# A recurrence's output projection and weight splits become steps of its own list; four products move to GpSimd

## The chip, the cores and the metric

One Trainium2 chip, one core of it. The metric is the device time of one execution of the whole program in microseconds (us). TensorE is called PE below, its weight loads PEld, VectorE DVE, ScalarE ACT, GpSimd POOL and the engine that issues most transfers SP.

## What is computed

The program is one inference step of a four-layer decoder trunk on 320 tokens (256 of a prompt, 64 of 8 samples), width 1024. Each layer is a token mixer (RG-LRU, Mamba-2, RWKV-7, RG-LRU) and then an MLP with squared ReLU. The change lies wholly in the third layer's mixer:

```python
def step(S, inp):                               # WKV recurrence, 16 heads of 64
    r_t, k_t, v_t, kk_t, a_t, w_t = inp
    sa = jnp.einsum("bhvk,bhk->bhv", S, kk_t)
    S = (S * w_t[:, :, None, :] - sa[..., None] * (kk_t * a_t)[:, :, None, :]
         + v_t[..., None] * k_t[:, :, None, :])
    return S, jnp.einsum("bhvk,bhk->bhv", S, r_t)
...
bonus = (jnp.sum(r_h * k_h * r_k, axis=-1, keepdims=True) * v_h).reshape(bsz, L, D_MODEL)
out = ((o + bonus) * g).astype(u.dtype)         # o: the steps' outputs, normed per head
return out @ w_out, u[:, -1], S_fin.astype(wkv0.dtype)
...
x = x + out.astype(x.dtype)
x = x + sqrelu_mlp(rmsnorm(x, p["norm_ffn"][layer]), ...)
```

## The kernel before

Everything is held feature-major, [128 partitions, 8 tiles, 320 tokens]. Weights come from HBM in chunks of 128x1024 f32 (512 KB) through three `wraw` buffers. Each chunk is split in two fp32r parts: ACT writes `whi` (a rounded copy), DVE writes `wlo` (the rest). There are three buffers of each, so a chunk's parts may be written when the matmuls of the third chunk before it have read theirs. A product with such a weight is three matmuls of 320 columns (whi with the high part of the activation, whi with the low part, wlo with the high part).

The recurrence (`wkv`, L1345) works on eight pairs of heads. For each pair there are chunks of 64 tokens: four of the prompt and one of the samples. Generators make its steps: `scores` and `operands` (products of the pair's tensors), `inverse` (a triangular inverse by doubling, blocks 1, 2, 4 ... 32; it needs `t`, a masked copy of `ar`, from block 2 on), `chain` (the four prompt chunks one after another), `chain_sample` (the samples' states: `spread` of vt and of sa, a product with the decay `dend`, then a transfer out), `output` and `finish` (norm, bonus `bs * vf`, gate, split into y's high part `ylw` and low part `yav`). The last two pairs are also prepared here.

What sets the order of all this is a planner, `Weave` (L326). Each step says which engine it wants, for how many ns by a table in the code, and which PSUM banks (six called `b`, one double bank `iu`). The planner keeps a clock for each engine, takes the step that could start first, and by a rank (`RANK`) among equals. What it takes is written out in that order and pinned: the engines run these instructions in program order. Instructions that aren't pinned are placed among them by the framework's scheduler, with a priority where the code gives one.

The output projection stands behind the planner's run. Its eight chunks (`OUT_CHUNKS`: four that hold pairs 0 to 3 of 256 output columns each, two that hold pairs 4 and 5 of 512, two that hold pairs 6 and 7 of 512) make 24 sums of [128, 320] in three PSUM banks, 192 matmuls in all, and each sum is added to the residual `x`. Three of the eight chunks are split as planned steps late in the recurrence (`weights`), the other five beside the projection, by `fill`:

```python
po = bank("b", m % 3)
for k in range(k0, k1):
    mm3(po[:, :N], w[0][:, k - k0, c], ...)
with tc.high_priority(60):
    V.tensor_tensor(x[:, m], x[:, m], po[:, :N], op=ALU.add)
if k1 == NT:
    nxt.tile(m)
```

`nxt.tile(m)` prepares the MLP's input from the finished tile m: ACT writes a square `nsq` (the first goes to `nacc` itself) and the scaled high part `xh`, DVE adds the square to `nacc` and writes the low part `xl`. The MLP's first product (`main_ps`) uses PSUM that the recurrence's banks held, so its first matmul waits for the last add to `x`.

## Time and profile before

| what | value |
|---|---|
| three runs | 1758.85, 1759.35, 1761.85 us, median 1759.35 |
| the profiled execution | 1755.34 us, of which the span 1753.3 |
| busy over the span | PE 97%, DVE 66%, ACT 56%, POOL 1% |
| recurrence, first matmul to the projection's first | 1024.41 to 1154.86 us |
| projection, first to last matmul | 1154.86 to 1185.03 us |
| MLP's first matmul | 1186.39 us |

All stretches below are us from the span's start. A row of the views by stretch gives each engine's busy time with the number of its instructions, then the granted share of TensorE's clock (1.00 is 2.4 GHz, 0.50 is 1.2 GHz). In the chain of waits the time is followed back from the last instruction, each piece under the line and engine that held it; "issue" is time in which the engine waited for nothing that the profile shows.

### The profile page before, as it was taken

The page shows a single profiled execution, that of the slowest core. Times are in us where ns is not written, and L with a number is a line of the kernel's source. Part 1 is how long each engine was busy: PE and PEld are TensorE (multiplying, and loading weights), DVE is VectorE, ACT ScalarE, POOL GpSimd, SP SyncE. Part 2 cuts the span into 40 slices and gives each one's busy share as a digit, 9 for nine tenths or more (in the row PEclk, how much of TensorE's full clock was granted, in tenths as well). Part 3 has the DMA queues.
Part 4 walks back from the last instruction along what each step waited for, and adds up shares of the span by engine and source line. Part 5 has one row for each costly group of instructions (what it writes and reads, how often), then busy time and mean ns, then how long its engine had stood idle before and what let it go on. Part 6 is the DMA issues. An engine that isn't in the chain of part 4 may idle for free.

```text
span 1753.3 us, 35969 instructions
## 1 busy us (share of the span) xinstructions
PE 1693.4 (97%) x15018; PEld 1635.1 (93%) x15018; DVE 1150.3 (66%) x1964; ACT 978.0 (56%) x1608; POOL 17.7 (1%) x36
## 2 busy tenths in 40 slices
PE   8999999989999999999999989899999999999997
PEld 7999999979999989999998977789999999999997
DVE  7975544499978976565467577786554469755444
ACT  7854443378857855553338566655543368554432
POOL 0000000000000000000000000000000000000000
PEclk9999999999999989999999999999999999999999
DMA  5444454545665534545434302134444444454452
GB/s 185 144 137 156 146 154 146 201 134 171 216 200 168 195 125 142 152 136 181 146 116 129 113 21 73 46 120 134 154 146 153 148 134 147 136 153 147 150 151 90
DMA packets 69746, 249.77 MB, mean 142 GB/s; under 512 B 9072, under 2 KB 11536, under 8 KB 67536
## 3 DMA queue, kind: packets, MB, share of 16 engines
q1 hardware_dynamic: 65040, 225.29, 41.5%
q0 software_dynamic: 2960, 18.89, 2.7%
q10 hardware_dynamic: 1584, 3.29, 0.5%
q8 instruction: 118, 1.93, 0.4%
q14 instruction: 44, 0.36, 0.1%
HBM read 233.52 MB, written 13.92 MB: 141 GB/s over the span
## 4 chain that ended last, share of the span: by engine, by line
PE 88%; DVE 7%; ACT 2%; issue 2%; DMA 1%; DVEq 0%; ACTq 0%
PE main_ps L498 22%; PE main_ps L500 22%; PE main_ps L499 22%; PE ps_b L1377 6%; PE aux_ps L499 2%; PE aux_ps L498 2%; PE aux_ps L500 2%; DVE wlo L495 1%; PE aux_ps L768 1%; DVE xc L792 1%; ACT whi L494 1%; PE ps_b L498 1%; PE ps_b L499 1%; PE ps_b L500 1%; PE ps_iu L1377 1%
## 5 line engine op out<-in xcount | busy, mean ns | idle before, releaser
L494 ACT ACTIVATE whi<-wraw 128x1024 fp32r<-128x1024 f32 x398 | 420.9, 1059 | 608.3 <-PE main_ps L499 512.4
L495 DVE TENSOR_TENSOR wlo<-wraw,whi 128x1024 fp32r<-128x1024 f32 x398 | 486.2, 1223 | 368.9 <-ACT whi L494 359.9
L498 PE MATMUL main_ps<-xh,whi 128*128 128x320 f32 x1664 | 521.4, 313 | 16.1 <-ACT whi L494 7.8
L499 PE MATMUL main_ps<-xl,whi 128*128 128x320 f32 x1664 | 518.8, 312 | 0.0
L500 PE MATMUL main_ps<-xh,wlo 128*128 128x320 f32 x1664 | 516.4, 310 | 0.9 <-DVE wlo L495 0.9
L498 PEld LDWEIGHTS main_ps<-xh,whi 128*128 128x128 f32 x1664 | 314.4, 189 | 18.4 <-ACT whi L494 8.0
L499 PEld LDWEIGHTS main_ps<-xl,whi 128*128 128x128 f32 x1664 | 314.3, 189 | 2.1 <-issue 0.4
L500 PEld LDWEIGHTS main_ps<-xh,wlo 128*128 128x128 f32 x1664 | 314.3, 189 | 2.0 <-DVE wlo L495 1.4
L500 PE MATMUL main_ps<-hh,wlo 128*128 128x320 f32 x768 | 237.2, 309 | 0.9 <-DVE wlo L495 0.9
L498 PE MATMUL main_ps<-hh,whi 128*128 128x320 f32 x768 | 237.0, 309 | 0.5 <-ACT whi L494 0.5
L499 PE MATMUL main_ps<-hl,whi 128*128 128x320 f32 x768 | 236.9, 309 | 0.0
L500 PEld LDWEIGHTS main_ps<-hh,wlo 128*128 128x128 f32 x768 | 144.0, 187 | 1.4 <-DVE wlo L495 1.4
L498 PEld LDWEIGHTS main_ps<-hh,whi 128*128 128x128 f32 x768 | 144.0, 187 | 0.8 <-ACT whi L494 0.8
L499 PEld LDWEIGHTS main_ps<-hl,whi 128*128 128x128 f32 x768 | 144.0, 187 | 0.0
L678 DVE SCALAR_TENSOR_TENSOR fr<-main_ps,nrs 128x640 f32<-128x640 f32 x64 | 52.7, 824 | 78.5 <-PE main_ps L500 78.5
L498 PE MATMUL aux_ps<-hh,whi 128*128 128x320 f32 x256 | 79.0, 309 | 0.0
L500 PE MATMUL aux_ps<-hh,wlo 128*128 128x320 f32 x256 | 79.0, 309 | 0.0
L499 PE MATMUL aux_ps<-hl,whi 128*128 128x320 f32 x256 | 79.0, 309 | 0.0
L495 DVE TENSOR_TENSOR hl<-fh,hh 128x640 fp32r<-128x640 f32 x64 | 52.8, 825 | 13.1 <-ACT hh L494 13.1
L851 DVE SCALAR_TENSOR_TENSOR cv<-sxb,k_b,cv 128x344 f32<-128x344 f32 x96 | 51.6, 569 | 0.8 <-ACT cv L849 0.8
L680 ACT ACTIVATE fh<-fr 128x640 f32<-128x640 f32 x64 | 47.3, 739 | 7.3 <-DVE fr L678 7.3
L662 DVE TENSOR_TENSOR x<-x,main_ps 128x320 f32<-128x320 f32 x56 | 24.8, 483 | 36.9 <-PE main_ps L500 36.9
(446 smaller groups left out, 2828.2 us busy)
## 6 DMA issues: line engine op xcount, KB each, us to landing
wraw<-in_wall SPq DMA_DIRECT2D x405, 512.0 KB, 3.7
ss<-in_s POOLq DMA_DIRECT2D x8, 1024.0 KB, 6.8
o_ssm_s<-ss POOLq DMA_DIRECT2D x8, 1024.0 KB, 4.3
acb<-acs_d SPq DMA_DIRECT2D x8, 640.0 KB, 3.9
wx<-in_k SPq DMA_DIRECT2D x8, 256.0 KB, 3.7
o_wkv_s<-wx SPq DMA_DIRECT2D x8, 256.0 KB, 2.7
o_ssm_p<-sp_o POOLq DMA_DIRECT2D x8, 128.0 KB, 4.3
wraw<-in_wlora SPq DMA_DIRECT2D x2, 512.0 KB, 3.7
```

What stands on the lines that cost most here:

```text
L494: S.activation(hi, src, AF.Copy)
L495: V.tensor_tensor(lo, src, hi.bitcast(F32), op=ALU.subtract)
L498: T.matmul(out, wh, ah, start=start, stop=False)
L499: T.matmul(out, wh, al, start=False, stop=False)
L500: T.matmul(out, wl, ah, start=False, stop=stop)
L662: ins = V.tensor_tensor(x[:, i], x[:, i], half(pt, m)[:, :N], op=ALU.add)
L678: V.scalar_tensor_tensor(r, pt[:, :, :N], 0.0, b2(prep.rs), op0=ALU.max, op1=ALU.mult)
L680: S.activation(h, r, AF.Square)
L768: T.matmul(pt[:, :NCV], w4[:, h % 4, s], xc[:, h, :NCV], start=True, stop=True)
L792: V.tensor_tensor_scan(xc[:, h, :NCV], ra[:, h], ix[:, h], 0.0, op0=ALU.mult, op1=ALU.add)
L851: V.scalar_tensor_tensor(out, src[:, k:k + NCV], w[k], out, op0=ALU.mult, op1=ALU.add)
L1377: return lambda *a, **k: tc.keep_in_program_order(fn(*a, **k))
```

## The change

The planner learns of a fourth engine, POOL, and of two kinds of step: `PM` (a PE step that changes between the recurrence's 64x64 matmuls and full ones, at 130 ns more) and `DV2` (a DVE step that reads two operands from SBUF), which it keeps from overlapping with POOL steps on its own clocks.

Four products a pair, 32 in all, go from DVE to POOL: the masked copy `t` (now a step `first` of its own, with a mark `m_t1` that the inverse waits for at block 2), the spread of vt, the samples' states times `dend`, and `bs * vf`. All eight chunks' loads and splits are planned steps (from the third pair's inverse on, at the earliest). The projection is eight planned generators, `project_out`; its adds to `x` lose their priority, are pinned, and any of the six banks may hold a sum. The `nxt.tile(m)` calls stand in a step `next_operand` but are not pinned. Several `RANK` values differ.

```diff
-    LAG = {"PE": 225, "ACT": 53, "DVE": 53, "SP": 0}
+    LAG = {"PE": 225, "ACT": 53, "DVE": 53, "POOL": 95, "SP": 0}
+    KIND = {"PM": "PE", "DV2": "DVE"}
+    SWITCH = 130
...
+                if ns and eng == "PE" and kind != self.mode:
+                    at += self.SWITCH
+                if kind in ("DV2", "POOL"):
+                    at = max(at, self.port)
...
-            RANK = (-27, -31, 0, -2, 21, 13, 36, -41, 30)
+            RANK = (-27, -31, -1, -9, 21, 20, 36, -55, 30, 30)
...
+            def first(g, ar, t):
+                yield "POOL", 680, ()
+                PG.tensor_tensor(t, ar, bc(vk("woff1t"), ND), op=ALU.mult)
+                wv.reach(g.m_t1)
...
-                yield "DVE", 420, ()
-                exv = spread(f"wexv{p % 2}", g.vt[:, j])
+                yield "POOL", 560, ()
+                exv = spread(PG, f"wexv{p % 2}", g.vt[:, j])
...
-                yield "DVE", 690, ()
-                PV.tensor_tensor(k0, k0, dend[:, p, 4:12].unsqueeze(2).to_broadcast([P, NB, 64]), op=ALU.mult)
+                yield "POOL", 1080, ()
+                PG.tensor_tensor(k0, k0, dend[:, p, 4:12].unsqueeze(2).to_broadcast([P, NB, 64]), op=ALU.mult)
...
+                yield g.m_ak
+                yield "POOL", 700, ()
+                PG.tensor_tensor(bs[:, p], bs[:, p], vf[:, p], op=ALU.mult)
...
-                for _ in range(3):
-                    yield gs[6].m_inv
+                yield prepared[7]
+                yield gs[2].m_inv
+                for j in range(len(jobs)):
+                    if j >= 3:
+                        yield w_out[j - 3]
                     raw = raw_chunk()
+                    yield "SP", 2500, ()
...
+            def project_out(j):
+                k0, k1, n, m0 = jobs[j]
+                for k in range(k0, k1):
+                    yield gs[k].m_fin
+                yield w_in[j]
...
+                    i, = yield "PM", 0, ("b",)
+                    po = bank("b", i)
+                    for k in range(k0, k1):
+                        if (k - k0) % 2 == 0:
+                            yield "PM", 882, ()
...
+                    yield "DVE", 490, ()
+                    PV.tensor_tensor(x[:, m], x[:, m], po[:, :N], op=ALU.add)
+                    wv.give("b", i)
+                    if k1 == NT:
+                        wv.add(200, next_operand(m))
...
-            for k0, k1, n in OUT_CHUNKS:
...
-                        with tc.high_priority(60):
-                            V.tensor_tensor(x[:, m], x[:, m], po[:, :N], op=ALU.add)
```

What this does to the order, at three places. **Where the projection begins, on PE.** `ylw`, `yav` are y's parts; rows of 64x64 are the recurrence's. Before, the projection's first matmuls stand behind all but two rows of the recurrence:

```order
L1377 MATMUL ps_b3_10627<-kr_9282,wsn12_11686 64x64 x2
L1377 MATMUL ps_b3_10627<-gbt1_10699,wsa13_11776 64x64 x2
L498 MATMUL ps_b1_10604<-ylw_11656,whi_13464 128x320
L499 MATMUL ps_b1_10604<-yav_11657,whi_13464 128x320
L500 MATMUL ps_b1_10604<-ylw_11656,wlo_13465 128x320
L1377 MATMUL ps_b5_10650<-kr_9282,k_c_9272 64x320 x2
```

Now they begin right behind the last pair's first prompt chunk:

```order
L1393 MATMUL ps_b0_10603<-kr_9282,wx_10597 64x2x8 x12
L1393 MATMUL ps_b5_10650<-vt1_10766,ht1_10938 64x64 x2
L1393 MATMUL ps_b5_10650<-wsa10_11408,bt1_11100 64x64 x2
L1393 MATMUL ps_b3_10627<-ylw_11675,whi_12073 128x320
L1393 MATMUL ps_b3_10627<-yav_11676,whi_12073 128x320
L1393 MATMUL ps_b3_10627<-ylw_11675,wlo_12074 128x320
```

Of the recurrence's 2792 matmuls 2788 stood ahead of the projection's first, now 2706; of the projection's 192, 7 stood ahead of the recurrence's last, now 120 (the first 60 in one piece), and 72 stand behind it.

**Where the projection ends, on DVE.** `x` are the adds to the residual, `nacc` and `xl` belong to `nxt.tile`, the `wlo` rows of L495 and L510 split the MLP's first chunks. Before, the last four adds and what follows:

```order
L1785 TENSOR_TENSOR x_72<-x_72,ps_b1_10604 128x320
L640 SCALAR_TENSOR_TENSOR xl_9268<-x_72,k_cm_73,xh_9267 128x320
L1785 TENSOR_TENSOR x_72<-x_72,ps_b2_10626 128x320
L1785 TENSOR_TENSOR x_72<-x_72,ps_b0_10603 128x320
L572 TENSOR_TENSOR nacc_9266<-nacc_9266,nsq_14259 128x320
L640 SCALAR_TENSOR_TENSOR xl_9268<-x_72,k_cm_73,xh_9267 128x320
L1785 TENSOR_TENSOR x_72<-x_72,ps_b1_10604 128x320
```

Now, up to the last add:

```order
L510 TENSOR_TENSOR wlo_14382<-wraw_14379,whi_14381 128x1024
L587 TENSOR_TENSOR nacc_9266<-nacc_9266,nsq_14284 128x320
L655 SCALAR_TENSOR_TENSOR xl_9268<-x_72,k_cm_73,xh_9267 128x320
L587 TENSOR_TENSOR nacc_9266<-nacc_9266,nsq_14295 128x320
L655 SCALAR_TENSOR_TENSOR xl_9268<-x_72,k_cm_73,xh_9267 128x320
L1393 TENSOR_TENSOR x_72<-x_72,ps_b0_10603 128x320
L587 TENSOR_TENSOR nacc_9266<-nacc_9266,nsq_14301 128x320
L655 SCALAR_TENSOR_TENSOR xl_9268<-x_72,k_cm_73,xh_9267 128x320
L1393 TENSOR_TENSOR x_72<-x_72,ps_b5_10650 128x320
L587 TENSOR_TENSOR nacc_9266<-nacc_9266,nsq_14313 128x320
L655 SCALAR_TENSOR_TENSOR xl_9268<-x_72,k_cm_73,xh_9267 128x320
L1393 TENSOR_TENSOR x_72<-x_72,ps_b4_10649 128x320
```

The split of the MLP's third chunk, `wlo_14382`, and what belongs to two finished tiles have moved ahead of the last three adds. On PE the projection's end and the MLP's beginning now read:

```order
L1393 MATMUL ps_b4_10649<-ylw_13906,whi_14215 128x320
L1393 MATMUL ps_b4_10649<-yav_13907,whi_14215 128x320
L1393 MATMUL ps_b4_10649<-ylw_13906,wlo_14216 128x320
L513 MATMUL main_ps_14342<-xh_9267,whi_14345 128x320
L514 MATMUL main_ps_14342<-xl_9268,whi_14345 128x320
```

`wlo_14216` is the projection's eighth chunk, and `wlo_14382`, three chunks later, is written into its buffer: it waits for the last matmul of the projection.

**Where the recurrence begins, on POOL.** Before, three copies are all that POOL does here:

```order
L1363 COPY ali0_10589<-k_c_9272 128x320
L1363 COPY ali1_10590<-k_c_9272 128x320
L1363 COPY ali2_10591<-k_c_9272 128x320
L443 DMA k_a1_16473<-in_k_a1 128x320
L826 DMA o_lru<-ob_16471 128x288
```

Now an instruction named ISA, which the build adds, and the products stand behind them:

```order
L1378 COPY ali2_10591<-k_c_9272 128x320
L1393 ISA
L1393 TENSOR_TENSOR wt10_10663<-war0_10661,k_c_9272 128x320
L1393 TENSOR_TENSOR wt11_10700<-war1_10698,k_c_9272 128x320
L1393 TENSOR_TENSOR bs_9284<-bs_9284,vf_9283 128x320 x2
L1393 TENSOR_TENSOR wx_10597<-vt0_10703,k_c_9272 128x256
```

The 32 products follow each other in one fixed order on POOL from there.

## Rows read from the trace of the kernel before

**Rows 1.** The page, busy time: engine, us (share of the span), instructions.
```profile
PE 1693.4 (97%) x15018; PEld 1635.1 (93%) x15018; DVE 1150.3 (66%) x1964; ACT 978.0 (56%) x1608; POOL 17.7 (1%) x36
```
**Rows 2.** Busy by stretch: stretch, length, PE, PEld, DVE, ACT, POOL, clock, DMA, GB/s.
```profile
1024.00:1145.00 121.00, 107.57 (x4022) 92.43 (x4023) 89.48 (x225) 80.40 (x241) 0.00 (x0) 0.99 0.17 54
1145.00:1155.00 10.00, 9.47 (x201) 6.85 (x200) 9.20 (x23) 7.58 (x27) 0.00 (x0) 1.00 0.28 86
```
**Rows 3.** Chain of waits, 1024 to 1145 us, shares by engine and line.
```profile
by line: PE ps_b L1377 72.6%; issue 11.0%; PE ps_iu L1377 7.5%; DVE whh L1377 2.0%; ACT wut L1377 1.6%; DVE wu L1377 0.8%; ACT gsq L1377 0.8%; ACT wxs L1377 0.7%; DVE wt L1377 0.4%; DVE gkt L1377 0.4%; DVE wsn L1377 0.4%; ACT wsa L1377 0.4%
```
**Rows 4.** Chain of waits, 1145 to 1185 us, shares by engine and line.
```profile
by line: PE ps_b L1377 27.0%; PE ps_b L498 24.4%; PE ps_b L499 23.2%; PE ps_b L500 22.8%; issue 1.4%; DVE nacc L572 1.2%; ACT wxs L1377 0.6%; ACT wsa L1377 0.6%; DVE x L1785 0.1%
```
**Rows 5.** DVE groups, 1024 to 1166 us: busy us, mean ns | idle before.
```profile
L1377 DVE TENSOR_TENSOR wx<-wx,dend 128x512 f32<-128x512 f32 x8 | 5.5, 690 | 0.2
L1377 DVE TENSOR_TENSOR wt<-war,k_c 128x320 f16<-128x320 f16 x8 | 3.9, 485 | 0.9 <-ACT war L1377 0.9
L1377 DVE TENSOR_TENSOR bs<-bs,vf 128x320 f32<-128x320 f32 x8 | 3.8, 480 | 0.0
L1377 DVE TENSOR_TENSOR wx<-vt,k_c 128x256 f32<-128x256 f32 x8 | 3.3, 415 | 0.0
```
**Rows 6.** Timeline of POOL: start, us, what.
```profile
1021.15 1.76 POOL L1363 COPY ali<-k_c 128x320 f32<-128x320 f32 x3 [375.59 <-DVE kk L1303]
```
**Rows 7.** Chain of waits in order of time, first doubling product.
```profile
1030.19 0.16 PE ps_iu L1377 x14
```
**Rows 8.** Timeline of PE around the projection's end.
```profile
1184.89 0.31 PE L499 MATMUL ps_b<-yav,whi 128*128 128x320 f32 x1
1185.03 0.30 PE L500 MATMUL ps_b<-ylw,wlo 128*128 128x320 f32 x1
1186.39 0.38 PE L498 MATMUL main_ps<-xh,whi 128*128 128x320 f32 x1 [1.05 <-DVE x L1785]
...
1191.01 0.39 PE L499 MATMUL main_ps<-xl,whi 128*128 128x320 f32 x1
1191.76 0.42 PE L500 MATMUL main_ps<-xh,wlo 128*128 128x320 f32 x1 [0.36 <-DVE wlo L495]
```
**Rows 9.** Timeline of DVE at the same place.
```profile
1179.00 1.23 DVE L495 TENSOR_TENSOR wlo<-wraw,whi 128x1024 fp32r<-128x1024 f32 x1 [0.46 <-ACT whi L494]
1180.14 1.28 DVE L1785 TENSOR_TENSOR x<-x,ps_b 128x320 f32<-128x320 f32 x3
...
1184.90 0.48 DVE L572 TENSOR_TENSOR nacc<-nacc,nsq 128x320 f32<-128x320 f32 x1
1185.31 0.55 DVE L640 SCALAR_TENSOR_TENSOR xl<-x,k_cm,xh 128x320 fp32r<-128x320 f32 x1
1185.77 0.48 DVE L1785 TENSOR_TENSOR x<-x,ps_b 128x320 f32<-128x320 f32 x1
```
**Rows 10.** Timeline of ACT at the same place.
```profile
1185.49 0.45 ACT L570 ACTIVATE nsq<-x 128x320 f32<-128x320 f32 x1
1185.85 1.04 ACT L494 ACTIVATE whi<-wraw 128x1024 fp32r<-128x1024 f32 x1
...
1187.16 0.55 ACT L639 ACTIVATE xh<-x,k_cm 128x320 fp32r<-128x320 f32 x1
```
**Rows 11.** Busy by stretch, as in rows 2, around two falls of the clock.
```profile
367.00:374.00 7.00, 2.91 (x20) 2.65 (x19) 6.74 (x16) 4.20 (x11) 0.00 (x0) 1.00 0.13 29
374.00:381.00 7.00, 5.47 (x21) 5.50 (x21) 6.66 (x12) 6.97 (x14) 0.00 (x0) 0.51 0.61 171
1080.00:1084.00 4.00, 2.99 (x137) 2.68 (x132) 3.21 (x9) 2.83 (x10) 0.00 (x0) 1.00 0.01 4
1084.00:1088.00 4.00, 4.00 (x80) 2.22 (x75) 2.10 (x7) 1.43 (x5) 0.00 (x0) 0.57 0.00 0
```
**Rows 12.** Timeline: a pair's variance product on PE, and its `ylw` on ACT.
```profile
1150.26 0.71 PE L1377 MATMUL ps_b<-gsq,k_c 64*64 64x320 f32 x4
...
1156.97 0.47 ACT L1377 ACTIVATE ylw<-cen 128x320 fp32r<-128x320 f32 x1 [0.22 <-DVE cen L1377]
```

More of the change, by code (lines that the diff above doesn't have):

```diff
@@ L404, in run @@
             at, _, task, took = best
-            eng, ns, _ = task.ask
+            kind, ns, _ = task.ask
+            eng = self.KIND.get(kind, kind)
+            if ns and eng == "PE":
+                self.mode = kind
+            if kind in ("DV2", "POOL"):
+                self.port = at + ns
             for tag, i in took:
@@ L1317, in prepare_steps @@
             wv.give("b", i)
-        yield "DVE", 820, ()
+        yield "DV2", 820, ()
         V.tensor_tensor_scan(L, vk("wkvreset"), lwp, 0.0, op0=ALU.mult, op1=ALU.add)
@@ L1422, in __init__ @@
                                             kr[:, 0, i], kr[:, 1, i]))
-                    for nm in ("ready", "a", "gbt", "vt", "ak", "ht", "gkt", "bt", "inv", "used", "o", "os", "out", "fin", "k0"):
+                    for nm in ("ready", "a", "gbt", "vt", "ak", "ht", "gkt", "bt", "inv", "used", "o", "os", "out", "fin", "k0", "t1"):
                         setattr(self, "m_" + nm, Mark())
@@ L1487, in inverse @@
                 PS.activation(ar, g.ali, AF.Copy)
-                yield "DVE", 490, ()
                 t = buf(f"wt1{j}", [P, ND, 64], F16)
-                PV.tensor_tensor(t, ar, bc(vk("woff1t"), ND), op=ALU.mult)
+                wv.add(g.i * 10 + RANK[1], first(g, ar, t))
                 u = None
@@ L1601, in chain_sample @@
                 both(pO, sa, g.gbt[:, j], False, True)
-                yield "DVE", 420, ()
-                exs = spread(f"wexs{p % 2}", sa)
+                yield "DV2", 420, ()
+                exs = spread(PV, f"wexs{p % 2}", sa)
                 yield "DVE", 220, ()
@@ L1763, in wkv, with next_operand @@
+            def next_operand(m):
+                yield "ACT", 930, ()
+                nxt.tile(m)
+                yield "DV2", 1040, ()
             prepared = {p: Mark() for p in (6, 7)}
@@ L1773, in wkv @@
             wv.add(75 + RANK[8], weights())
+            for j in range(len(jobs)):
+                wv.add(75 + RANK[9] + j, project_out(j))
             wv.run()
[L1775 to L1787 removed]
     prep = Prep("norm_mix0")
```

65 lines of the change are left out of this document (36 added, 29 removed).

## The prediction

> **What bounds the kernel now.** I read the page first [rows 1]: PE is busy in 97% of the span, and DVE in two thirds of it. That average says little of this change, which touches one stage, so the stretches of that stage come next [rows 2]. In the recurrence proper, 1024 to 1145 us, PE is busy for 107.57 of 121 us, DVE for 89.48, ACT for 80.40, POOL for nothing. From 1145 us on PE is full (9.47 of 10). The chain of waits tells what PE's idle time hangs on. In the body 72.6 + 7.5 = 80.1% of it is PE itself, 11.0% is "issue", and the remaining 8.9%, or .089 x 121 = 10.8 us, is DVE and ACT together [rows 3]. From 1145 to 1185 us the PE lines alone make 97.4%, and 2.6% of 40 us, about 1 us, is anything else [rows 4]. So the body has 10.8 us that faster DVE work could touch at most, the projection about 1 us, and the hand-over to the MLP a gap that can be read instruction by instruction [rows 8 to 10].
>
> **The change part by part.** *Four products a pair leave DVE.* They measured .485, .415, .690 and .480 us, eight each: 8 x 2.07 = 16.6 us [rows 5], 18.5% of DVE's 89.48. What this frees is DVE's queue. Of the products themselves the chain's listed lines hold only `wt`, .4% of 121, or .5 us [rows 3]; the rest of the gain must come from chain steps (`whh`, `wu`, `gkt`, `wsn`) that no longer stand behind a product. In exchange `t` and the spread of vt become two hand-overs to another engine, on an engine whose only rows here are three copies in 1.76 us, .59 each, with one input [rows 6]. Five more weight chunks' `wlo` come into the list, at a pitch of 1.14 us (1179.00 to 1180.14 [rows 9]), and so give 5.7 of the 16.6 us back. DVE would then have about 79 of 121 us, ACT with five more `whi` of 1.04 [rows 10] about 86, and PE still is the busiest. The gain can't exceed the 10.8 us; a loss is possible, since each of eight inverses waits for a POOL product that may be longer than .485: eight times, say, .6 us gives +5. I take -2.5, nearest to the listed `wt` row and about a fifth of the whole share, because the products' own rows are so little of the chain. Kept for the range: -10.8 to +5.
>
> *POOL's first product* has cover. POOL is free at 1021.15 + 1.76 = 1022.91 [rows 6], and the first doubling product, which needs `t`, runs at 1030.19 [rows 7]: 7.3 us for the added ISA instruction and one product. Cost nothing; if the two take longer, the excess is paid once.
>
> *Projection matmuls move forward.* 120 instead of 7 of the 192 stand ahead of the recurrence's last matmul. They could fill PE's idle time, but they move into a stretch where PE hardly has any [rows 2, 4]: of the 2.6% I expect half a microsecond, -.5 (0 to -1). The 130 ns changes of matmul kind exist on the planner's clock; no row shows such a cost, and the mixed stretch from 1145 us holds PE at 97.4% all the same.
>
> *The last pair's y.* Its parts are needed 24 matmuls behind its variance product in the new order, 24 x .14 = 3.4 us by the pitch of [rows 8]. Before, the way from such a product to `ylw` took 1156.97 - 1150.26 = 6.7 us with DVE as loaded as it was [rows 12]. So PE waits between 0 and 3.3 us there, and for the eighth chunk's `wlo`, which stands behind adds on the same queue. I take a third, +1.1, because fewer operations stand between now.
>
> *The hand-over to the MLP* is the main term. Before, the last projection matmul starts at 1185.03, the last add at 1185.77, and the MLP's first matmul at 1186.39: 1.36 us [rows 8, 9]. The adds came early, since their priority put them ahead of the tiles' preparation. Now they are pinned, and the split of the MLP's third chunk and two tiles' `nacc` and `xl` stand ahead of the last three adds on DVE. `wlo_14382` is written over the chunk that the projection's last matmul reads, and its `whi` over one that the last but one reads, so this piece of DVE's queue can't move until the projection has ended. From the start of that last matmul: its `whi` ends at about +1.25 (the matmul before it ends, then 1.04 [rows 10]); `wlo` 1.14 more, to +2.39; then `nacc` .41 (1184.90 to 1185.31), `xl` .46 (to 1185.77) [rows 9], both twice, 1.74 in all, so the add to the first of the three tiles starts at +4.13. Then each add sends its tile through ACT and back before the next add may go: add .48 [rows 9], a hand-over of about .1, `nsq` at a pitch of .36 (1185.49 to 1185.85), `xh` .55 [rows 10], and `xl` .46: 1.95 a round. Two rounds bring the last add to +8.05. From an add's start to the MLP's first matmul it is .62 (1185.77 to 1186.39): +8.7 where it was 1.36, so 7.3 us more, and 8.1 if DVE comes to this place .8 late with the splits of the two chunks before. One thing is given back: before, PE waited at 1191.76 for the second chunk's `wlo` (.75 us from start to start instead of .14 [rows 8]), and that chunk is split by then now: -.6. Net +6.7 to +7.5, and I take +7.1. Nothing hides this: PE has no other work ahead of the MLP.
>
> *The clock behind it.* Where PE was busy for 2.91 of 7 us at clock 1.00, the following stretch shows .51 with 5.47 us busy; where it was busy for 2.99 of 4 us, the next four show .57 [rows 11]. These are TensorE's two levels, 2.4 and 1.2 GHz, mixed in the slice. The second cost 4.00 x .43 = 1.7 us of PE time, the first 5.47 x .49 = 2.7. An idle hole of 8.7 us is likely to bring such a fall to the MLP's first matmuls. I take +1.7, range 0 to +2.7.
>
> **The sum**: -2.5 - .5 + 1.1 + 7.1 + 1.7 = +6.9 us. The profiled execution took 1755.34, so this one would take 1762.2; it lay 4.0 below the median of the runs, 1759.35, which gives 1766.2. I forecast 1766.
>
> **The rivals.** *The relief is larger than the hole.* If the chain's DVE and ACT steps are late mainly by queueing, taking a fifth of DVE's load away could clear most of the 10.8 us. For it: the many short DVE steps between PE's (`whh` alone 2.0% [rows 3]) and DVE's 74% load in the body [rows 2]. Against it: DVE idles for 31 of the 121 us, and of 16.6 us moved 5.7 come back. It decides from a relief of 5.9 us on: the time is then under 1762.9. With the full 10.8 it is 1766.2 - 8.3 = 1757.9, no change; if in addition the clock doesn't fall behind the hole (-1.7), y is never late (-1.1), the hole is at its lower end (-.4) and the projection gains its whole microsecond (-.5), it is 1754.2, faster.
>
> *POOL and DVE block each other.* The change itself keeps these products apart from DVE's steps with two operands in SBUF, by its planner's clocks; but the engines run by semaphores, and nothing in the program enforces that distance. If one in four of the 32 products holds a DVE step, or is held by one, for as long as a product took on DVE (mean 2.07 / 4 = .52 [rows 5]), and each such hold reaches PE, it is 32 x .25 x .52 = +4.2, so 1770.4. For it: DVE's 74% load leaves few gaps. Against it: no row of before has both engines at work, so this one is open; POOL's work is in one fixed order, and its products read tensors that are ready long before.
>
> The Trainium skill (SBUF — State Buffer, section Who interferes with whom) has a rule for this: a DVE instruction with two SBUF inputs contends with a GpSimd instruction that reads SBUF, and whichever issues first keeps the shared ports for its whole length while the other fully blocks. By that rule this rival is the rule's own price wherever the planner's clocks miss; if they always hit, it costs nothing. No run here shows it yet.
>
> *The change doesn't do what it says*, in that the adds and `nxt.tile` don't run in the written order: the order of instructions on DVE is fixed in the built program, so I give this nothing.
>
> **How the numbers follow.** A chance of .50 for the forecast, .32 for the relief, .18 for the ports. The forecast and the ports are slower by over 0.2% (3.5 us, about what a measurement of this kernel can tell from no change), above 1762.9: .68. Of the relief's .32 I give .22 to a time within 0.2%, 1755.8 to 1762.9, and .10 to faster. For the range, all terms at their favourable ends give 1759.35 + (-10.8 - 1.0 + 0 + 6.7 + 0) = 1754.3, and at their other ends 1759.35 + (5 + 0 + 3.3 + 7.5 + 2.7) = 1777.9. Neither is likely as a whole. 1757 leaves a tenth out below, 1773 a tenth above.
>
> **What would show it.** The start-to-start gap between the projection's last matmul and the MLP's first: 8.7 to 9.5 us instead of 1.36, with DVE's three last adds each about 2 us behind the other and idle time ended by ACT between them; it is wrong if the gap is under 4. A stretch of clock near .5 right behind. DVE's busy time from the recurrence's first matmul to 1145 us down by some 10 us or more, while the chain's share on DVE and ACT falls only from 8.9 to about 7%; below 4% the relief has won. The "issue" share should stay near 11%. Products on POOL that start as soon as their inputs are there, and DVE rows with two SBUF operands no longer than before; such rows growing to more than a microsecond would mean the ports. The first `t` should end before the matmuls that stood at 1030.19 want it. The largest error would be in the relief, which is the only term that rests on a share and not on single instructions.

## The result, and the profile after

The changed kernel takes 1768.99 us (median of five runs, 1768.14 to 1771.52), the kernel before 1758.85 in the same comparison: a ratio of 1.0057, with a 95% interval from 1.0043 to 1.0071. It is slower by 10 us. 1766 was forecast, within 1757 to 1773.

The profiled execution has a span of 1766.4 us where that of before had 1753.3, 13.1 us more. Read from stage to stage, the difference comes to: .9 us ahead of the recurrence (its first matmul starts at 1025.30 instead of 1024.41, in code that the change doesn't touch), 2.2 us from there to the projection's last matmul (162.8 instead of 160.6), 8.45 us in the gap behind it, and 1.6 us from the MLP's first matmul on. The page's busy times, as in [rows 1]:

```profile
PE 1696.3 (96%) x15018; PEld 1639.0 (93%) x15018; DVE 1138.3 (64%) x1932; ACT 978.6 (55%) x1608; POOL 46.1 (3%) x68
```

The products have moved: POOL is busy for 28 us more and DVE for 12 us less. The gap is on PE's timeline, which answers to [rows 8]:

```profile
1187.96 0.31 PE L1393 MATMUL ps_b<-yav,whi 128*128 128x320 f32 x1
1188.11 0.30 PE L1393 MATMUL ps_b<-ylw,wlo 128*128 128x320 f32 x1
1197.92 0.61 PE L513 MATMUL main_ps<-xh,whi 128*128 128x320 f32 x1 [9.51 <-DVE x L1393]
1198.33 0.47 PE L514 MATMUL main_ps<-xl,whi 128*128 128x320 f32 x1
1198.60 0.47 PE L515 MATMUL main_ps<-xh,wlo 128*128 128x320 f32 x1
...
1203.04 0.31 PE L514 MATMUL main_ps<-xl,whi 128*128 128x320 f32 x1
1203.19 0.31 PE L515 MATMUL main_ps<-xh,wlo 128*128 128x320 f32 x1
```

From the projection's last matmul to the MLP's first PE waits 9.81 us from start to start (1.36 before), and what ended the wait is an add to `x` on DVE. Then the matmuls follow each other every .27 us (1198.33 to 1198.60), and from 1203 on every .15. The stretches around the gap, columns as in [rows 2], show why:

```profile
1188.00:1198.00 10.00, 0.49 (x4) 0.26 (x3) 8.59 (x17) 5.12 (x11) 0.00 (x0) 0.73 0.42 122
1198.00:1203.00 5.00, 5.00 (x19) 5.00 (x20) 1.01 (x2) 0.80 (x2) 0.00 (x0) 0.51 0.02 3
1203.00:1208.00 5.00, 5.00 (x38) 5.00 (x37) 1.23 (x1) 1.71 (x2) 0.00 (x0) 1.00 0.18 32
```

PE was busy for .49 of 10 us, and in the 5 us behind it the granted clock was .51: TensorE's lower level, 19 matmuls where the next 5 us hold 38. What DVE did in those 10 us, to be held against [rows 9]:

```profile
1189.64 0.88 DVE L1393 TENSOR_TENSOR x<-x,ps_b 128x320 f32<-128x320 f32 x2
1190.44 1.22 DVE L510 TENSOR_TENSOR wlo<-wraw,whi 128x1024 fp32r<-128x1024 f32 x1
1191.58 0.48 DVE L587 TENSOR_TENSOR nacc<-nacc,nsq 128x320 f32<-128x320 f32 x1
...
1193.30 0.48 DVE L1393 TENSOR_TENSOR x<-x,ps_b 128x320 f32<-128x320 f32 x1
1194.38 0.49 DVE L587 TENSOR_TENSOR nacc<-nacc,nsq 128x320 f32<-128x320 f32 x1 [0.59 <-ACT nsq L585]
1194.83 0.55 DVE L655 SCALAR_TENSOR_TENSOR xl<-x,k_cm,xh 128x320 fp32r<-128x320 f32 x1
1195.30 0.48 DVE L1393 TENSOR_TENSOR x<-x,ps_b 128x320 f32<-128x320 f32 x1
...
1197.30 0.48 DVE L1393 TENSOR_TENSOR x<-x,ps_b 128x320 f32<-128x320 f32 x1
```

This is the piece of the written order that the section on the change showed: the split of the MLP's third chunk at 1190.44, then `nacc` and `xl` of two tiles, and three adds that stand 2.00 us apart (1193.30, 1195.30, 1197.30), each round with a wait for ACT.

### The profile page after: what moved, and what is told of

Read it like the earlier page. It is cut to its first block, busy times and chain, and to the rows that moved or that the text cites. A ratio compares the mean times of both kernels' runs of the same rounds, so it can differ in the third digit from the quotient of the medians.

```text
span 1766.4 us, 35983 instructions
## 1 busy us (share of the span) xinstructions
PE 1696.3 (96%) x15018; PEld 1639.0 (93%) x15018; DVE 1138.3 (64%) x1932; ACT 978.6 (55%) x1608; POOL 46.1 (3%) x68
## 4 chain that ended last, share of the span: by engine, by line
PE 87%; DVE 7%; issue 2%; ACT 2%; DMA 1%; DVEq 0%; ACTq 0%; POOLq 0%
PE main_ps L513 22%; PE main_ps L515 22%; PE main_ps L514 22%; PE ps_b L1393 7%; PE aux_ps L514 2%; PE aux_ps L513 2%; PE aux_ps L515 2%; DVE wlo L510 1%; PE aux_ps L783 1%; DVE xc L807 1%; DMA k_b<-in_k_b 1%; PE ps_iu L1393 1%; PE st_ps L1116 0%; PE nrm_ps L610 0%; ACT whi L509 0%
## 5 line engine op out<-in xcount | busy, mean ns | idle before, releaser
L509 ACT ACTIVATE whi<-wraw 128x1024 fp32r<-128x1024 f32 x393 | 415.4, 1058 | 599.0 <-PE main_ps L514 519.7
L510 DVE TENSOR_TENSOR wlo<-wraw,whi 128x1024 fp32r<-128x1024 f32 x393 | 480.3, 1223 | 373.0 <-ACT whi L509 364.1
L510 DVE TENSOR_TENSOR hl<-fh,hh 128x640 fp32r<-128x640 f32 x64 | 52.8, 825 | 12.7 <-ACT hh L509 12.7
L509 ACT ACTIVATE hh<-fh 128x640 fp32r<-128x640 f32 x64 | 47.4, 741 | 2.0
```

The lines of the kernel that those rows point to most:

```text
L509: S.activation(hi, src, AF.Copy)
L510: V.tensor_tensor(lo, src, hi.bitcast(F32), op=ALU.subtract)
```

## Experiments on the gap

**The adds first.** In the kernel `tailfix` the list, the early splits and the POOL products stay, and only the end is changed:

```diff
-                    PV.tensor_tensor(x[:, m], x[:, m], po[:, :N], op=ALU.add)
+                    if k1 == NT:
+                        with tc.high_priority(60):
+                            V.tensor_tensor(x[:, m], x[:, m], po[:, :N], op=ALU.add)
+                    else:
+                        PV.tensor_tensor(x[:, m], x[:, m], po[:, :N], op=ALU.add)
...
                 for m in range(m0, m0 + n // P):
+                    if j == 7 and m - m0 in (1, 3):
+                        fill(1 + (m - m0) // 2)
```

> The changed kernel with the last eight adds to x given back their priority and unpinned, and the split of the MLP's first two chunks asked for beside the last projection chunk; the list, the early splits and the POOL products stay. In the changed kernel's trace PE stands still for 9.81 us from start to start between the projection's last matmul and the MLP's first (1.36 before), and the MLP's first 18 matmuls then run at a pitch of .267 instead of .147 us, 2.2 us more. Theory (the hole by the order of DVE's last adds): the gap falls to about 1.4 us, the clock stays at 1.00, a wait of up to 1 us for the second chunk's wlo comes back, and the time falls by 9 to 10 us to 1759 or 1760. Rival (the MLP can't use an earlier start, since its weights' splits or the tiles' low parts come late anyway): the gap only moves to the MLP's third and following matmuls, time 1765 or more. Either way the body (first recurrence matmul to last projection matmul, 162.8 us against 160.6 before) stays as it is in the changed kernel.

Measured: 1760.55 us, the kernel before 1760.68 in the same comparison, ratio 1.0002 (.9990 to 1.0014). PE's timeline of this kernel:

```profile
1191.19 0.30 PE L1393 MATMUL ps_b<-ylw,wlo 128*128 128x320 f32 x1
1192.16 0.38 PE L513 MATMUL main_ps<-xh,whi 128*128 128x320 f32 x1 [0.67 <-DVE x L1820]
1192.39 0.31 PE L514 MATMUL main_ps<-xl,whi 128*128 128x320 f32 x1
1192.53 0.31 PE L515 MATMUL main_ps<-xh,wlo 128*128 128x320 f32 x1
```

The gap is .97 us, and the matmuls behind it run at .15 us. By the ratios, 1.0057 against 1.0002, the end of the projection cost 9.7 us. The expected 9 to 10 came, so the loss of the change lies there, and all the rest of it, the list, the early splits and POOL, adds up to nothing measurable (by this ratio's interval between 1.8 us less and 2.5 more). Two things of the expectation didn't come: PE has no wait for the second chunk's `wlo`, and the stretch from the recurrence's first matmul to the projection's last is 165.5 us in this profile, not the 162.8 of the changed kernel (the section on the products takes this up).

**Only the priority.** `addsfirst` has the first half of that diff without the two calls of `fill`.

> The changed kernel with only the priority of the last eight adds given back; the split of the MLP's first chunk isn't asked for early. On DVE wlo of that chunk now stands behind all tiles' nacc and xl. Theory (the start of the MLP is the sum of DVE's order, whatever it is): the first MLP matmul follows at 1.4 us or less, but the third, which reads that wlo, waits for about an xl, four times nacc and xl (.46 + 4 x .87 = 3.9 us) and the split (1.2 us), so it comes some 5 us late, at 6 to 7 us from the projection's last matmul; the time is 4 to 5 us above tailfix, 1765, and 4 below the changed kernel. Rival (the priority of the adds alone was the cause): as tailfix, 1760.5.

Measured: 1763.62 us, ratio 1.0018 (1.0006 to 1.0030), 3 us above `tailfix` where 4 to 5 were expected. By the times alone the two intervals overlap; the PE timeline tells the two kernels apart. It has the wait where it was expected, behind the first matmuls:

```profile
1192.83 0.38 PE L513 MATMUL main_ps<-xh,whi 128*128 128x320 f32 x1 [0.67 <-ACT nsq L585]
...
1195.05 0.41 PE L513 MATMUL main_ps<-xh,whi 128*128 128x320 f32 x1 [1.69 <-ACT whi L509]
1195.30 0.31 PE L514 MATMUL main_ps<-xl,whi 128*128 128x320 f32 x1
1197.79 0.63 PE L515 MATMUL main_ps<-xh,wlo 128*128 128x320 f32 x1 [0.52 <-DVE wlo L510]
```

The projection's last matmul starts at 1191.85 here, so the first product with `wlo` comes 5.9 us behind it; in `tailfix` that is 1.3. PE uses a part of the time for matmuls without `wlo`, which the sum had left out. It had left out the clock too: from 1198.23 to 1203.29 the matmuls stand .27 us apart, some 2.3 us more than at .15. From the projection's last matmul to the end of the span this profile has 572.9 us and that of `tailfix` 568.9. An add that comes early is worth little while the next thing that PE needs stands behind the same tiles on DVE.

**The same fault without the list.** `beforepin` is the kernel before with one thing of the change: its adds lose the priority and are pinned.

```diff
-                        with tc.high_priority(60):
-                            V.tensor_tensor(x[:, m], x[:, m], po[:, :N], op=ALU.add)
+                        PV.tensor_tensor(x[:, m], x[:, m], po[:, :N], op=ALU.add)
```

> The kernel before with one thing of the change: the adds to x lose their priority and are pinned. No product on POOL, no list for the projection. On DVE the split wlo_14382 of the MLP's third chunk, one nacc and one xl now stand between the last but one add and the last. Theory (the hole is the sum of what stands ahead of the last add on DVE from the moment that the projection's end frees the split's buffers): whi done at +1.25 us from the last projection matmul's start, wlo to +2.39, nacc .41 and xl .46 to +3.26, then .62 to the MLP's first matmul: a gap of 3.9 us instead of 1.36, and none of the .6 us at the second chunk; time 1.9 us above the kernel before. The changed kernel's 9.81 us would then be the same sum with two more tiles. Rival (the hole comes from the list, which ends with late sums): the gap stays at 1.4 us and the time equals that of before.

Measured: 1773.49 us, ratio 1.0082 (1.0065 to 1.0099). The gap, on PE, and what filled it, on DVE:

```profile
1192.28 0.31 PE L500 MATMUL ps_b<-ylw,wlo 128*128 128x320 f32 x1
1196.20 0.61 PE L498 MATMUL main_ps<-xh,whi 128*128 128x320 f32 x1 [3.62 <-DVE x L1377]
```

```profile
1193.57 1.23 DVE L495 TENSOR_TENSOR wlo<-wraw,whi 128x1024 fp32r<-128x1024 f32 x1
1194.71 0.49 DVE L572 TENSOR_TENSOR nacc<-nacc,nsq 128x320 f32<-128x320 f32 x1
1195.12 0.55 DVE L640 SCALAR_TENSOR_TENSOR xl<-x,k_cm,xh 128x320 fp32r<-128x320 f32 x1
1195.58 0.48 DVE L1377 TENSOR_TENSOR x<-x,ps_b 128x320 f32<-128x320 f32 x1
```

The gap is 3.92 us where the sum over DVE's order gave 3.9. The time was expected 1.9 above before and is 14 above. The waits of PE in the projection (1155 to 1193 us) show a second price of late adds, which the expectation had not seen:

```profile
PE ps_b L498 <- DVE x L1377: 4.3, 3, 1.9
```

The three PSUM banks of this kernel come free only with the adds, so late adds stop the projection too (three times, 4.3 us); it takes 36.7 us (1155.59 to 1192.28) instead of 30.2. A third price is the clock: behind two of the waits, from 1188.70 to 1191.37 and from 1196.61 to 1201.41, the matmuls stand .27 us apart, some 3.4 us more in all than at .15. In the changed kernel, with six banks, PE's only waits in the projection are .54 us for `wlo` and .20 for `yav`; that the banks are the reason was not tried. The sum for the gap is confirmed, the sum for the time was not complete; and this kernel's single profiled execution, 1767.04 us, is itself 6 us under its median.

**The clock.** `dummies` is the changed kernel with 56 matmuls behind the projection's last, into a bank that nothing reads:

```diff
             wv.run()
+            po, y = bank("iu", 0), yhl[3][0][:, 1]
+            for k in range(56):
+                PT.matmul(po[:, 0, :N], y[:, :P], y, start=k == 0, stop=k == 55)
```

> The changed kernel with 56 matmuls of 320 columns, 8.2 us at .147 each, on PE behind the projection's last matmul, into a bank that nothing reads. They fill PE's hole and change no wait. Theory (the clock behind the hole falls because PE stood idle): granted clock 1.00 in the MLP's first 5 us, pitch .147, the first main_ps matmul at the same distance from the projection's end (about 9.8 us), time 2.2 us less than the changed kernel, 1766 to 1767. Rival (the fall comes from the change of stage, not from idling): clock stays at .5 for the first 18 matmuls, time 1769 as now.

Measured: 1769.15 us, ratio 1.0046 (1.0030 to 1.0062) against 1.0057 for the changed kernel. The times differ by 2 us with intervals that overlap, and the expected 1766 to 1767 did not come as a figure (the kernel before had 1760.68 in this comparison); what the clock did is settled by the trace. The added matmuls and the MLP's first on PE, and the 5 us from there on by stretch:

```profile
1192.46 8.37 PE L1393 MATMUL ps_iu<-ylw 128*128 128x320 f32 x56
1202.13 0.38 PE L513 MATMUL main_ps<-xh,whi 128*128 128x320 f32 x1 [1.30 <-DVE x L1393]
```

```profile
1202.00:1207.00 5.00, 4.87 (x33) 4.90 (x34) 1.14 (x3) 1.99 (x3) 0.00 (x0) 1.00 0.00 0
```

The MLP's first matmul is as late as in the changed kernel (9.82 us behind the projection's last), but the clock behind it is 1.00 and 33 matmuls stand where 19 stood. From the MLP's first matmul to the end of the span it takes 565.7 us instead of 568.5. So the fall comes from PE standing idle, and costs 2 to 3 us beside the gap's own 8.45.

## Experiments on the products and the list

**POOL alone.** `poolonly` has the four products on POOL and the changed ranks; the projection stands behind the planner's run as before. The parts that differ from the changed kernel:

```diff
-            for j in range(len(jobs)):
-                wv.add(75 + RANK[9] + j, project_out(j))
             wv.run()
+            for k0, k1, n in OUT_CHUNKS:
+                for m0 in range(0, NT, n // P):
...
+                        with tc.high_priority(60):
+                            V.tensor_tensor(x[:, m], x[:, m], po[:, :N], op=ALU.add)
```

> The four products on POOL and the changed ranks, but the projection and five of the splits behind the planner's run as before. Theory (relief of DVE is worth 2.5 us, as in the prediction): body about 158 us, time 1756 to 1757. Rival one (ports): DVE rows with two SBUF inputs lengthen and the body stays at 160 to 162, time 1759 to 1761. Rival two (relief is larger): body 154 or less, time 1752 or less.

Measured: 1760.30 us, ratio .9994 (.9983 to 1.0005). That is between 3.0 us faster and .9 slower: neither the 2.5 nor the ports' rival can be told from nothing, and the larger relief (1752 or less) is excluded. The stretch from the recurrence's first matmul to the projection's last fits none of the three: 166.4 us in the profile, where 158, 160 to 162 or at most 154 were expected.

**POOL undone in the same plan.** A new plan moves everything (below), so `tailsameplan` keeps the plan and the order of `tailfix`, PE's row for row, and changes only who executes the products:

```diff
-            PT, PS, PV, PG = (Pinned(e) for e in (T, S, V, nc.gpsimd))
+            PT, PS, PV, PG = (Pinned(e) for e in (T, S, V, V))
```

> The kernel of tailfix (1760.55 us) with one word changed: where the plan puts the four products on POOL, VectorE executes them, at the same places of the written order. PE's order is the same, row for row. This undoes POOL alone, which a new plan (taildve) could not. Theory (the relief of DVE is small, as poolonly's ratio of 0.9994 to before says): DVE's busy time in the body rises by 16.6 us less the 2 us by which holds stretch it now, the time rises by 1 to 4 us, 1761.5 to 1764.5. Rival one (the relief is large, but the list ate it): 1766 or more. Rival two (POOL's slower products, mean .79 to 1.20 us, and the holds cost as much as the relief brings): within 1 us of 1760.55.

Measured: 1759.38 us, ratio 1.0000 (.9987 to 1.0014); `tailfix` had 1.0002. The theory's 1 to 4 us more did not come; the result is nearest to the second rival, in which the relief and POOL's price cancel. Moving 16.6 us from DVE to POOL shows no gain: the two ratios differ by .4 us, known to some 3.5 us to either side. `tailmixed`, the same plan with the two products on POOL that PE doesn't wait for soon, says the same.

```diff
+            PL = Pinned(nc.gpsimd)
...
-                PG.tensor_tensor(k0, k0, dend[:, p, 4:12].unsqueeze(2).to_broadcast([P, NB, 64]), op=ALU.mult)
+                PL.tensor_tensor(k0, k0, dend[:, p, 4:12].unsqueeze(2).to_broadcast([P, NB, 64]), op=ALU.mult)
...
-                PG.tensor_tensor(bs[:, p], bs[:, p], vf[:, p], op=ALU.mult)
+                PL.tensor_tensor(bs[:, p], bs[:, p], vf[:, p], op=ALU.mult)
```

> The plan of tailfix once more, with two of the four products on POOL (the samples' states times dend, and bs*vf, which nothing on PE waits for soon) and two on VectorE (t, which the inverse waits for, and the spread of vt). Theory (in the recurrence PE is held by its own instruction fetch, whose pieces stand some 3.5 us apart in the chain of waits, so that time taken from DVE's share comes back as issue): within 2 us of tailfix and tailsameplan, 1758 to 1762, with DVE, ACT and issue together 24 to 25 of 120 us of the chain as in all of them. Rival (POOL's gain was hidden by the two products that PE waits for): 1757 or less, with the sum of the three at 22 or less.

Measured: 1759.27 us, ratio 1.0001 (.9988 to 1.0014), as the theory had it. Its second half failed: DVE, ACT and issue together hold 28.2 of the 120 us in its profile (7.4, 4.8 and 16.0), where before, the changed kernel, `tailfix` and `tailsameplan` have 23.6 to 23.8. Of this, 2.6 us are the start: until 1028.40 its chain runs over the preparation on DVE and ACT (`kk`, `av`, `ali`, `war`), where the others have PE. Without them it is 25.6, still 2 us more.

Where the relief may have gone is read from the chain of waits over 120 us from the recurrence's first matmul, to be held against [rows 3]. First the changed kernel, then `tailfix`, then `tailsameplan`:

```profile
by line: PE ps_b L1393 72.6%; issue 12.0%; PE ps_iu L1393 7.7%; ACT wut L1393 1.8%; DVE wlo L1393 0.9%; ACT whi L1393 0.8%; DVE ali L1393 0.4%; DVE wu L1393 0.4%; DVE whh L1393 0.4%; DVE gkt L1393 0.4%; DVE whu L1393 0.4%; ACT war L1393 0.4
```

```profile
by line: PE ps_b L1393 72.1%; issue 13.0%; PE ps_iu L1393 8.1%; ACT wut L1393 1.8%; DVE wlo L1393 0.9%; ACT whi L1393 0.8%; DVE ali L1393 0.4%; DVE whh L1393 0.4%; DVE wu L1393 0.4%; DVE gkt L1393 0.4%; ACT war L1393 0.4%; ACT bt L1393 0.4%
```

```profile
by line: PE ps_b L1393 72.6%; issue 10.1%; PE ps_iu L1393 7.7%; DVE whh L1393 1.2%; DVE wx L1393 1.2%; ACT wut L1393 1.2%; DVE wu L1393 1.1%; DVE whu L1393 1.0%; DVE wt L1393 0.7%; DVE wsn L1393 0.5%; DVE ak L1393 0.4%; ACT bt L1393 0.4%; D
```

With the products on DVE, its steps do stand in the chain: added up piece by piece, DVE holds 9.0 of the 120 us in `tailsameplan`, 7.4 in `tailmixed` and 3.2 in `tailfix`, so the relief that the prediction spoke of is there. But "issue", in which PE waits for nothing that the trace shows, goes the other way: 12.1, 16.0 and 15.6 us. What DVE no longer holds up, the instruction supply seems to. `tailmixed` doesn't fit well: it has as much issue as `tailfix` and, without its start (1.8 us of DVE), 5.6 us of DVE. The second rival's reason, that holds and POOL's slower products eat the relief, is not excluded: POOL itself holds nothing in any of these chains, but what the holds add to DVE's steps was not tried. (These sums cut the pieces at the edges of the stretches that were read; the numbers in some expectations count those twice and are up to 1.4 us higher.)

How far single profiles can be trusted here was tried with two second profiles. The kernel before again (`beforecopy`):

> The kernel before once more, unchanged, for a second profile. The profile of before that the prediction used lay 4 us below the median of its runs. If its body (160.6 us from the recurrence's first matmul to the projection's last) is typical, this one shows 160 to 162 us and the POOL kernels' 163 to 166 us are a loss of 2 to 5. If the body itself varies between executions, through the pieces that the chain calls issue (13.2 of 120 us in the first profile, 15.2 to 16.9 in the POOL kernels), this one shows 163 to 166 with issue above 15.

It showed 160.56 us from the recurrence's first matmul to the projection's last (160.62 in the first profile), with 14.7 us of issue (13.2) and 4.2 of DVE (4.9). And `tailsameplan` again (`sameplancopy`):

> The kernel of tailsameplan once more, for a second profile. Its first profile shows 159.8 us from the recurrence's first matmul to the projection's last and 12.7 of 120 us as issue in the chain of waits, tailfix (the same PE order, products on POOL) 165.5 us and 16.9; but the medians of the two are within 1.2 us. If POOL's products cost PE's instruction supply 4 us, this profile shows 159 to 161 us and issue of 12 to 14 again, and the medians' equality stays unexplained. If it is the spread of single executions, it shows something between, 161 to 166 us, with issue above 14.5.

It showed 162.6 us (159.8), 13.6 of issue (12.1) and 7.2 of DVE (9.0), between the two expectations; its time was .9993 of before (.9979 to 1.0007). So one kernel's profiles can lie 2.9 us apart in this stretch, with the same exchange between DVE and issue. An estimate from two rows puts more than half of the 2.9 us down to the clock, which fell in the second profile and not in the first. The same four microseconds, columns as in [rows 2], `sameplancopy` first, then `tailsameplan`:

```profile
1082.00:1086.00 4.00, 3.67 (x83) 3.29 (x84) 1.86 (x5) 1.29 (x3) 0.00 (x0) 0.59 0.02 6
```

```profile
1082.00:1086.00 4.00, 3.48 (x128) 3.31 (x128) 2.34 (x7) 2.00 (x5) 0.00 (x0) 1.00 0.04 9
```

At .59 instead of 1.00 these 4 us are worth 4.00 x .41 = 1.6 us less. Six profiles with products on POOL (the changed kernel, `tailfix`, `poolonly`, `dummies`, `addsfirst`, `tailmixed`) lie at 162.8 to 166.4 us with 14.4 to 16.1 of issue, four without (before and `tailsameplan`, twice each) at 159.8 to 162.6 with 12.1 to 14.7. Each of the six has at least one such fall of the clock there (`tailfix` two: .67 from 1050 to 1054 us, .66 from 1074 to 1078), of the four only two have one. And by their times `tailfix`, `poolonly`, `tailmixed` and `tailsameplan` all lie between .9993 and 1.0002 of before. So it is not shown that POOL raises issue by some 2 us: these are single profiles, and their clocks differ too. What three comparisons show is that the time doesn't fall by more than the noise.

**New plans.** Three kernels change what the planner plans. `taildve` is `tailfix` with the products planned as DVE steps, `tailnoport` without the distance between POOL's and DVE's steps, and `tailsplitlate` with the weight splits from the sixth pair's inverse on:

```diff
-                yield "POOL", 680, ()
-                PG.tensor_tensor(t, ar, bc(vk("woff1t"), ND), op=ALU.mult)
+                yield "DV2", 490, ()
+                PV.tensor_tensor(t, ar, bc(vk("woff1t"), ND), op=ALU.mult)
```

> The kernel of tailfix with the four products back on DVE: the list without POOL. The planner makes another order of it. Theory (the body's extra 2.2 us come from the five weight splits in the list, which stood 2.6 us in the chain of waits at 1101 us, and not from POOL): the body is as long as in the changed kernel or longer by up to 3 us, since DVE has 16.6 us more to do; time 1759 to 1763. Rival (POOL products and DVE rows with two SBUF inputs hold each other, which costs the body 2 us or more): the body falls to 160 us or below, time 1757 or less.

```diff
-                if kind in ("DV2", "POOL"):
-                    at = max(at, self.port)
```

> The kernel of tailfix (1760.55 us), where the planner no longer keeps POOL's products apart from DVE's steps with two SBUF operands. Theory (the distance on the planner's clocks doesn't survive on the chip, where in the changed kernel the product wx<-wx,dend took 1.04 us five times but 1.44 and 1.90 as well): DVE rows with two SBUF operands and POOL rows lengthen no more than in tailfix, time within 3 us of it, 1758 to 1763. Rival (the distance works and holds would cost without it): those rows lengthen clearly, cen above .63 and .62 us, the POOL products above .89 and 1.20 us in the mean, and the time is above 1764.

```diff
-                yield gs[2].m_inv
+                yield gs[5].m_inv
```

> The kernel of tailfix (1760.55 us), with the weight splits of the list allowed only from the sixth pair's inverse on instead of the third's. Theory (the split's 1.1 to 1.9 us in the chain of waits at 1101 us and again later are paid, because ACT's whi and DVE's wlo stand in front of a chain step): the body is 1 to 2 us shorter, time 1758.5 to 1759.5. Rival (they only fill waiting time that the instruction fetch causes anyway): time equal within 1 us.

Measured: 1766.74 us (ratio 1.0032, 1.0020 to 1.0043), 1767.55 (1.0056, 1.0043 to 1.0068) and 1765.17 (1.0036, 1.0023 to 1.0049). All three are slower than `tailfix`, by their ratios by 5 to 10 us. `taildve` and `tailsplitlate` lie above all that was expected of them; only the rival of `tailnoport` had a time above 1764. Much of the loss is not what they were meant to test: each new plan sets a new order for the end of the recurrence. The 45 us from 120 to 165 us behind the recurrence's first matmul by stretch, `tailfix` first, then `tailnoport`, then `tailsplitlate`:

```profile
1145.66:1190.66 45.00, 44.27 (x544) 38.66 (x541) 31.60 (x63) 22.69 (x58) 6.66 (x7) 1.00 0.26 79
```

```profile
1147.77:1192.77 45.00, 39.40 (x487) 32.82 (x486) 27.15 (x53) 17.19 (x46) 4.27 (x3) 0.93 0.27 85
```

```profile
1145.11:1190.11 45.00, 39.35 (x422) 33.52 (x420) 27.13 (x53) 16.90 (x39) 2.20 (x2) 0.95 0.32 98
```

PE is idle for 5 us more there, and the clock is lower. The longest single waits of PE in that stretch (`tailnoport`, `tailsplitlate`):

```profile
PE ps_b L1391 <- ACT ylw L1391: 2.4, 1, 2.4
```

```profile
PE ps_b L1393 <- ACT ylw L1393: 4.4, 1, 4.4
```

This is the term "the last pair's y" of the prediction, near and above its upper end of 3.3: the projection has used up everything else, and PE waits for the last pair's norm and gate. `taildve` has the same wait, 2.3 us; PE is busy for 40.67 of the same 45 us there, at clock .93. So none of the three says what its edit costs. In `tailnoport` the held rows do lengthen as its rival said (`cen` times `gz` .669 us in the mean instead of .575, `bs` on POOL 1.046 instead of .891), but by the sum of all such rows that adds up to some 2 to 3 us on two engines, and what of it reaches PE isn't known; the idle end is 5 us.

## Why the prediction was right, and where it wasn't

**The hand-over to the MLP**, +7.1 forecast, came out as the main term, by the mechanism and at the place that were named; it measured 8.45 in the gap less the .6 at the second chunk (no wait for `wlo` stands in the MLP's first product any more), so 7.9, .4 above the upper end. The gap was forecast as 8.7 to 9.5 us and is 9.81. From `wlo_14382` on the sum holds within a tenth: 6.86 us from its start to the last add's, 6.80 forecast (its terms add up to +8.03 for the last add, not +8.05, so 6.78). What was too small is DVE's lateness at that point. The sum let it come there at +1.25 us, or .8 later; it came at +2.33, because the split of the second chunk had itself waited for ACT, whose `whi` had waited 1.63 us for the projection's matmuls (to 1186.55):

```profile
1187.64 1.23 DVE L510 TENSOR_TENSOR wlo<-wraw,whi 128x1024 fp32r<-128x1024 f32 x1 [1.29 <-ACT whi L509]
```

**The clock**, +1.7 forecast: 2.2 measured, 18 matmuls at .267 instead of .147 us. That it falls because of the hole was tried with `dummies`.

**The last pair's y and the eighth chunk's `wlo`**, +1.1 forecast: PE waited .20 us for `yav` and .54 for `wlo`, .7 in all. The upper end of 3.3 was no exaggeration: other orders of the same list pay 2.4 and 4.4 for `ylw` alone.

**The relief of DVE**, -2.5 forecast, is the term that did not come, as the prediction's last sentence feared. DVE's busy time in 120 us fell from 88.5 to 80.2 us, by 8.4 where some 10 were forecast, and the chain's time on DVE and ACT in them from 10.3 to 9.2 us, to 7.7%, where about 7% was forecast. But "issue" didn't stay: 13.2 us became 14.4. In time no relief shows: `poolonly` lies between 3.0 us faster and .9 slower than before, and `tailfix` and `tailsameplan` are equal within some 3.5 us. Neither alone excludes 2.5 us, and nothing shows them; why they are missing is open between the instruction supply and the holds. Read with the projection's part (-.5), the recurrence and projection were to be 1.9 us shorter and were 2.2 longer in the profile; by the ratio of `tailfix`, about unchanged. The forecast of +6.9 against +10 measured is this (1.9), the hand-over (.8) and the clock (.5).

**The rivals.** The large relief didn't come. Of the ports, the trace shows the holds and their size. POOL's products without one, and with one, beside what DVE did at the time (first POOL's row, then DVE's, at each of two places):

```profile
1108.07 1.90 POOL L1393 TENSOR_TENSOR wx<-wx,dend 128x512 f32<-128x512 f32 x1 [12.21 <-PE ps_iu L1393]
```

```profile
1107.85 1.22 DVE L1393 TENSOR_TENSOR wlo<-wraw,whi 128x1024 fp32r<-128x1024 f32 x1
```

```profile
1070.15 0.79 POOL L1393 TENSOR_TENSOR wt<-war,k_c 128x320 f16<-128x320 f16 x1 [2.84 <-ACT war L1393]
```

```profile
1070.41 0.87 DVE L1393 TENSOR_TENSOR wprep<-wprep,av 128x320 f32<-128x320 f32 x1
```

At 1108 DVE's split was there first, kept its usual 1.22 us, and POOL's product took 1.90 instead of the 1.04 that six of the eight take; at 1070 POOL was first and kept its .79, and DVE's product took .87 instead of .48. The rule that the prediction quoted from the Trainium skill (SBUF — State Buffer, section Who interferes with whom) is what these two places show: whichever starts first goes on as if alone, and the other one waits. Of 32 products seven were held, for 2.6 us, and five DVE instructions for 1.9 us in all. That is twelve holds and 4.5 us where the rival had eight and 4.2, and one DVE row passed the microsecond that was named as its sign (`cen` times `gz` at 1095.19, 1.02 us instead of .49). So the holds came in full, and the planner's distance did not prevent them. What did not come is that each of them reaches PE: in `tailfix`, with the products on POOL as well, all of the change but its end costs .4 us by the ratio (from 1.8 less to 2.5 more). How much of the holds a relief pays for in that sum isn't known.

**POOL's first product** ran at 1027.35, and the second `t` behind it ended at 1028.93; the first matmul that reads `t` ran at 1031.01. So the cover held, the ISA instruction included. (Before, that first matmul ran at 1029.86; 1030.19, which the prediction took, is the longest piece of the doubling in the chain.)

```profile
1027.35 1.58 POOL L1393 TENSOR_TENSOR wt<-war,k_c 128x320 f16<-128x320 f16 x2 [3.55 <-ACT war L1393]
```

No version beat the kernel before: `tailfix`, `tailsameplan`, `tailmixed` and `poolonly` all lie within .2% of it.

## What to carry to other kernels

Where an operation that the next stage waits for changes from placed by priority to written in a fixed order, write down what stands ahead of it on its engine from the moment at which the slowest of these can start: here this sum gave the gap within 1.1 us, and in a second kernel within .1. A planner's list that ends with a stage should contain what the next stage needs, its first splits too, or must leave the last operations free to be moved. To learn what an engine's share is worth, keep the written order and change only who executes it: a new plan moved the time by 5 to 10 us, and the edit in the kept order by nothing that could be measured.

## What the runs showed of the hardware

The pieces that the chain calls issue are not evenly spread, but come at a steady pitch where PE hardly waits for another engine. In the changed kernel's first 20 us of the recurrence:

```profile
1030.08 0.51 issue
...
1033.36 0.95 issue
...
1037.09 0.68 issue
...
1040.59 0.63 issue
```

They stand 3.3 to 3.7 us apart, and 3.3 to 4.0 in the kernel before (1028.67, 1032.65, 1036.20, 1039.49, 1043.24). What lies between two of them is the same number of instructions on PE, 128 matmuls and 128 weight loads:

```profile
1030.08:1033.36 3.28, 2.76 (x128) 2.68 (x128) 2.16 (x6) 1.88 (x5) 1.06 (x2) 1.00 0.04 7
1033.36:1037.09 3.73, 2.79 (x128) 2.67 (x128) 1.20 (x4) 2.27 (x6) 0.00 (x0) 1.00 0.02 4
```

This goes on through the recurrence. Of the 14.4 us of issue in the changed kernel's 120 us, 13.0 are 18 pieces of .3 to 1.8 us that all stand a multiple of 256 matmuls and weight loads apart; in the kernel before it is 10.5 of 13.2 us in 16 pieces, on the same grid of 256 counted from the kernel's start. Over 120 us the DMA view has 31 packets of .51 MB together on the queue for instructions, so one of 16 KB for every 3.9 us:

```profile
q8 instruction: 31, 0.51, 1.8%
```

The same 120 us hold 3970 matmuls and 3972 weight loads, 31 times 256. So most of issue is a stop of PE where the next 256 of its instructions begin. With many small matmuls (4022 in 107.57 us of busy PE [rows 2], 37 a microsecond) the supply of instructions thus comes near to being the next bound behind DVE and ACT, which would explain where the relief went: a PE that comes to the next stop earlier waits there longer. That it is the bound was not tried.
